# One decoder step on one core: activations written unsplit and split after reading, next round's first products between this round's, key sums queued later

## The chip, the cores and the metric

The kernel runs on one core of a Trainium2 chip. The metric is the device time of one execution in microseconds. A core has a matrix engine (TensorE, PE in the profile, whose weight loads are listed as PEld), three engines that work on tiles in on-chip memory (VectorE or DVE, ScalarE or ACT, GpSimd or POOL), and a queue that only issues transfers (SyncE, SP). Transfers (DMA) are issued from SP and, in this kernel, from ScalarE's own queue; such an issue stands in ScalarE's order like any of its instructions. Each engine works through its own list in order.

## The reference

One layer of a hybrid decoder on 2048 prompt tokens and 8 x 4 sample tokens, model width 1024:

```python
q, k, v, z, xbc, dt_raw = project(x, norm_mix, w_in)          # RMSNorm(x) @ w_in
att = three dilated window attentions, combined by their softmax denominators
ssd = ssd_mixer(z, xbc, dt_raw, ...)                          # Mamba-2 scan, gated RMSNorm
h = x + concat(att, ssd) @ w_out
gu = rmsnorm(h, norm_ffn) @ w_gate_up                         # 1024 -> 2 * 2816
y = rmsnorm(h + (silu(gu[..., :D_FF]) * gu[..., D_FF:]) @ w_down)
# sample tokens: their keys and values are the cached ones and the four new ones
sc = einsum('bshd,bsjhd->bhsj', q, k_gathered) * scale        # scores over <= 129 keys
```

It returns the two outputs and the new caches and states. All inputs and outputs are float32.

## The kernel before, in words

A float32 product is made of three faster ones. Each operand is split in two `float32r` tiles: `hi` is a rounded copy (ScalarE), `lo` the difference (VectorE), and a product is hi.hi + hi.lo + lo.hi (`mm3`, L108 to L110).

The prompt is worked in two halves of 1024 tokens. Each half runs projection, attention and scan for two blocks of 512 tokens, then the output projection, then two stages that the change touches:

1. **Rounds** (gate and up projection, `rest`, L1443 to L1476). The 2816 columns are 22 pieces `f` of 128. A piece is a 2 x 2 block product done with seven instead of eight block products: operands x11, x21, xt2, xt1, xt3, x22, xt4 (rows as `mm<-x11h` in the profile). A product is 12 matmuls (`product`, L1419). Half 0 has 22 rounds of 512 columns; half 1 also takes the sample tokens along and has 44 rounds of 264 columns, two per piece. The first two products of a round (x11 into a bank of PSUM named `mm`, x21 into one named `s`) are its lead, done by `lead_mm` at the start of the round before. `lead_ev` evacuates it: ScalarE copies x11 into `e[0]` (L1438), VectorE adds x21 (L1439), ScalarE applies SiLU (L1440). The tile `ev` has four parts, e0 to e3, and its pool has two buffers. `rest` does the other five: t2 onto the same `mm` bank, copied to e1 (L1449); t1 into a bank `o`, copied to e3 (L1453); t3 onto `mm` (L1456 adds it to e3, L1457 copies it to e2); 22 onto `o` (L1461, SiLU L1462, product L1463); t4 into a bank `t` (L1467, L1468). PSUM has two banks of each name. At the end `ev` is split (L1472 hi, L1473 lo) and both halves are written to memory as `hiD` and `loD` (L1475) from ScalarE's queue. Between the products, weights of the next pieces are split (`split_unit`, L1378, L1379).

2. **Down projection** (`down`). The 22 rows of `w_down` come in groups `g` of 2, 2, 3, 3, 3, 3, 3, 3. While group g is multiplied, group g+1's activations are read back from `hiD` and `loD` (L1505) and its weights are loaded and split (`split`, L1510 hi, L1511 lo). A group goes over 8 blocks `i` of 128 tokens, two banks each (`t` and `o`); VectorE adds each into `acc` (L1614), in group 0 ScalarE copies (L1616). Tiles of the activations are used again two groups later, so a load for g+1 waits for the end of g-1.

In half 0 the sample tokens' scan and attention run between the blocks of the down projection (`sample_parts`): every block gives credits, eight credits run one step. The steps of a branch are eight keys, one set of weights, eight values. A key step (`keys`, one sample sequence) multiplies cached keys by the broadcast query rows on GpSimd (L1003, 1024 numbers per partition), adds the halves of each head on GpSimd (L1005, 512 numbers) and sums the rest on VectorE (L1006). `weights` then transposes the scores on TensorE (L1014) and makes the softmax. The tiles `sk` come from a pool of eight (`SLOTS`); their loads, from the cache and from `qD`, are issued on ScalarE's queue.

The order on each engine is not the order of the source: a scheduler with its own cost model puts the instructions in an order when the program is built, source order being its priority. `behind(...)` (L122) and `issue_after` tie an instruction behind others in that order.

Of the kernel before, what the change touches and what calls it, by code (L numbers as in the profile page):

```python
# [8 lines left out]
F = mybir.dt.float32  # L9
R = mybir.dt.float32r  # L10
# [23 lines left out]
def hybrid_step(ctx: ExitStack, tc: tile.TileContext, x_prompt, x_sample, cache_kv_d1, cache_kv_d4,  # L34
# [34 lines left out]
    hiD = dram.tile([DFF, 2, TQ + NS // 2], F, name="hiD")  # L69
    loD = dram.tile([DFF, 2, TQ + NS // 2], F, name="loD")  # L70
# [762 lines left out]
    def sample_steps():  # L833
# [164 lines left out]
        def keys(br, b):  # L998
            def f(kvp, sm):
                nk = (128, 128, 64)[br]  # L1000
                kt, qb = W.pop((0, br, b))
                kk = kt[:, 0:1].to_broadcast([128, 4, 256]) if br == 0 else kt[:nk]
                nc.gpsimd.tensor_tensor(qb[:nk], qb[:nk], kk, op=OP.mult)  # L1003
                q4 = qb[:nk].rearrange("p s (h d) -> p s h d", h=4)
                nc.gpsimd.tensor_tensor(q4[:, :, :, :32], q4[:, :, :, :32], q4[:, :, :, 32:], op=OP.add)  # L1005
                nc.vector.tensor_reduce(sT[:nk, 4 * b:4 * b + 4], q4[:, :, :, :32], axis=mybir.AxisListType.X, op=OP.add)  # L1006
            return f

# [86 lines left out]

        yield ssd_pre
# [21 lines left out]
        for br in range(3):  # L1118
            for b in range(8):
                yield use(keys(br, b))  # L1120
            yield weights(br)
            for b in range(8):
                yield use(values(br, b))
# [35 lines left out]
    def half_step(half, X, right):  # L1159
# [265 lines left out]
        def lead_mm(r):  # L1425
            f, c0, n = r
            a11, a12 = U["a", f]
            b1 = bank("mm")
            product(b1, a11, "11", c0, n, True)
            b2 = bank("s")  # L1430
            product(b2, a12, "21", c0, n, True)
            U[r] = b1, b2

        def lead_ev(r):
            f, c0, n = r
            b1, b2 = U[r]
            ev = evp[0].tile([128, 4, TQ], F, name="ev")
            nc.scalar.copy(ev[:, 0, :n], b1[:, :n])  # L1438
            nc.vector.tensor_add(ev[:, 0, :n], ev[:, 0, :n], b2[:, :n])  # L1439
            nc.scalar.activation(ev[:, 0, :n], ev[:, 0, :n], AF.Silu)  # L1440
            U[r] = ev, b1

        def rest(j, between):  # L1443
            f, c0, n = r = rounds[j]
            s2, s1, s3, s4, a22 = U["b", f]
            ev, b1 = U.pop(r)
# [7 lines left out]
            between()  # L1454
            product(b1, s3, "t3", c0, n, False)
            v = nc.vector.tensor_add(e[3], e[3], b1[:, :n])  # L1456
            a = nc.scalar.copy(e[2], b1[:, :n])  # L1457
            with behind([v.ins, a.ins] if j == len(rounds) - 1 else ()):
                between()
            product(b3, s4, "22", c0, n, False)  # L1460
# [10 lines left out]
            hi, lo = ev[:, 0:2, :n], ev[:, 2:4, :n]  # L1471
            nc.scalar.activation(hi.bitcast(R), lo, AF.Copy)  # L1472
            nc.vector.tensor_tensor(lo.bitcast(R), lo, hi, op=OP.subtract)  # L1473
            for t, p in ((hiD, hi), (loD, lo)):
                dma2.dma_start(t[128 * f:128 * f + 128, :, c0:c0 + n], p)  # L1475
# [4 lines left out]
        def down_load(g):  # L1480
# [9 lines left out]
            def load():  # L1490
                for j in range(n):
# [12 lines left out]
                    for t, d in zip(a, (hiD, loD)):  # L1504
                        asked[:] = [dma.dma_start(t.bitcast(F).rearrange("p (b t) -> p b t", b=2),  # L1505
                                                  d[128 * f:128 * f + 128, :, :TQ]).ins]
# [18 lines left out]
            return ([load] + first if g == 1 else first + [load]), [lambda j=j: split(j) for j in range(n)], out  # L1525
# [28 lines left out]
        for k in range(2):  # L1554
            lead_ev(rounds[k])
        for j, r in enumerate(rounds):
# [5 lines left out]
            if 0 < j < len(rounds) - 1:  # L1562
                lead_mm(rounds[j + 1])
                lead_ev(rounds[j + 1])
# [17 lines left out]
            act = rest(j, between)  # L1582
# [18 lines left out]
        def down(g, ws, nw, after=None):  # L1601
            for f in nw[0]:
                f()
            for i in range(8):
# [4 lines left out]
                for nh in range(2):  # L1609
# [3 lines left out]
                    if g:  # L1613
                        add = nc.vector.tensor_add(acc[i][:, ns], acc[i][:, ns], ps)  # L1614
                    else:
# [168 lines left out]
```

## Time and profile before

| | us |
|---|---|
| median of the runs (3163.44 to 3173.74) | 3168.82 |
| profiled execution, device time | 3155.93 |
| its span, first to last instruction | 3154.2 |
| TensorE busy | 3007.1 (95%) |
| VectorE, ScalarE, GpSimd busy | 1759.6, 1285.3, 501.4 |

In the profile the rounds of half 0 run from about 815 to 1237 us, its down projection from there to 1600; the rounds of half 1 from 2388 to 2886, its down projection to the end. TensorE's time is nearly the kernel's time, so the page is read for where TensorE stands still and what ended each wait. A busy TensorE can still be slow: the granted clock (1.00 is 2.4 GHz) says at which speed it ran.

### The profile page before, as it was taken

What the parts mean: (1) busy time and instruction counts of PE and PEld (TensorE: products, weight loads), DVE (VectorE), ACT (ScalarE), POOL (GpSimd) and SP (SyncE); (2) the same over time, 40 slices, a digit from 0 to 9 for tenths busy, and PEclk for the clock granted to TensorE, in tenths of its full rate; (3) what the DMA queues carried; (4) which work ended last, traced back from release to release, by engine and by line L of the source; (5) the groups of instructions that cost most, each with busy time, mean ns of one, the idle gap of its engine ahead of it and who ended that gap; (6) DMA issues with size and microseconds to landing.
All of it is one profiled execution on the core that took longest, in us unless ns stands there. A gap on an engine that the chain in (4) does not pass through costs nothing.

```text
span 3154.2 us, 47095 instructions
## 1 busy us (share of the span) xinstructions
PE 3007.1 (95%) x18563; PEld 2498.9 (79%) x18563; DVE 1759.6 (56%) x3381; ACT 1285.3 (41%) x2636; POOL 501.4 (16%) x371
## 2 busy tenths in 40 slices
PE   7999999999999998988999999999998999999999
PEld 7889877787678787666676788777777999998777
DVE  3359623786665653644443596237856565663434
ACT  3466424663444443211144564246634444443001
POOL 1000100012332320045330000000013222220101
PEclk9899999999999999889999999999998999999999
DMA  4333444352344346559545344443433343335432
GB/s 131 93 85 108 155 133 121 89 168 98 114 147 147 134 152 245 161 181 304 139 158 145 84 117 147 148 131 90 148 113 107 118 129 125 105 106 202 151 136 102
DMA packets 457570, 431.31 MB, mean 137 GB/s; under 512 B 55652, under 2 KB 383996, under 8 KB 456836
## 3 DMA queue, kind: packets, MB, share of 16 engines
q1 hardware_dynamic: 295216, 260.02, 26.6%
q10 hardware_dynamic: 162132, 168.28, 16.8%
q8 instruction: 146, 2.39, 0.3%
q14 instruction: 76, 0.62, 0.1%
HBM read 346.14 MB, written 109.22 MB: 144 GB/s over the span
## 4 chain that ended last, share of the span: by engine, by line
PE 56%; DMA 6%; DVE 6%; POOL 4%; ACT 2%; issue 2%; ACTq 0%; POOLq 0%; DVEq 0%; SPq 0%
PE mm L1419 9%; PE o L1419 6%; PE mm L110 4%; PE mm L108 4%; PE mm L109 4%; PE t L1419 3%; PE s L1419 3%; PE t L108 2%; PE t L109 2%; PE t L110 2%; PE o L109 2%; PE o L108 2%; PE o L110 2%; DMA loD<-ev 2%; POOL sk L1003 1%
## 5 line engine op out<-in xcount | busy, mean ns | idle before, releaser
L108 PE MATMUL mm<-xh,hi 128*128 128x512 f32 (+1 forms) x1280 | 467.2, 365 | 3.0 <-ACT xh L147 2.4
L110 PE MATMUL mm<-xh,lo 128*128 128x512 f32 (+1 forms) x1280 | 463.0, 362 | 1.1 <-DVE lo L95 1.1
L109 PE MATMUL mm<-xl,hi 128*128 128x512 f32 (+1 forms) x1280 | 459.8, 359 | 1.0 <-DVE xl L148 1.0
L95 DVE TENSOR_TENSOR lo<-raw,hi 128x1024 fp32r<-128x1024 f32 x200 | 247.3, 1237 | 233.3 <-ACT hi L94 232.6
L94 ACT ACTIVATE hi<-raw 128x1024 fp32r<-128x1024 f32 x200 | 211.1, 1057 | 299.3 <-PE mm L109 121.9
L108 PEld LDWEIGHTS mm<-xh,hi 128*128 128x128 f32 x1280 | 245.2, 192 | 41.0 <-issue 7.5
L110 PEld LDWEIGHTS mm<-xh,lo 128*128 128x128 f32 x1280 | 244.6, 191 | 39.5 <-issue 4.9
L109 PEld LDWEIGHTS mm<-xl,hi 128*128 128x128 f32 x1280 | 245.4, 192 | 35.7 <-issue 3.4
L711 POOL TENSOR_TENSOR sq<-sq,acc 128x512 f32<-128x512 f32 (+2 forms) x25 | 35.6, 1425 | 1228.9 <-ACT acc L710 645.6
L1614 DVE TENSOR_TENSOR acc<-acc,t 128x512 f32<-128x512 f32 x112 | 76.7, 685 | 116.0 <-PE t L110 115.8
L591 DVE SCALAR_TENSOR_TENSOR acc<-u,cw,acc 128x512 f32<-128x512 f32 x168 | 125.6, 747 | 3.6 <-ACT acc L589 1.8
L1614 DVE TENSOR_TENSOR acc<-acc,o 128x512 f32<-128x512 f32 x112 | 76.6, 684 | 84.6 <-PE o L110 84.5
L108 PE MATMUL mm<-hi,xh 128*128 128x256 f32 (+3 forms) x408 | 115.5, 284 | 0.7 <-ACT vt L481 0.7
L110 PE MATMUL mm<-hi,xl 128*128 128x256 f32 (+3 forms) x408 | 116.0, 285 | 0.0
L109 PE MATMUL mm<-lo,xh 128*128 128x256 f32 (+3 forms) x408 | 115.9, 284 | 0.0
L356 ACT ACTIVATE p<-p,st 128x256 f32<-128x256 f32 (+4 forms) x192 | 83.8, 440 | 62.6 <-DVE st L354 56.1
L1472 ACT ACTIVATE ev<-ev 128x528 fp32r<-128x528 f32 (+1 forms) x66 | 51.8, 784 | 121.8 <-DVE ev L1468 112.6
L1620 POOL TENSOR_TENSOR acc<-acc,hr 128x1024 f32<-128x1024 f32 x16 | 40.0, 2498 | 351.7 <-DVE acc L1614 340.4
L1510 ACT ACTIVATE hi<-raw 128x1024 fp32r<-128x1024 f32 x22 | 23.0, 1059 | 170.6 <-DVE acc L1614 101.8
L1473 DVE TENSOR_TENSOR ev<-ev 128x528 fp32r<-128x528 f32 (+1 forms) x66 | 65.2, 988 | 39.2 <-ACT ev L1472 38.3
L1456 DVE TENSOR_TENSOR ev<-ev,mm 128x264 f32<-128x264 f32 (+1 forms) x66 | 33.8, 513 | 89.9 <-PE mm L1419 86.1
L108 PE MATMUL o<-hi,ah 128*128 128x512 f32 x176 | 72.2, 410 | 7.6 <-DVE acc L1614 7.6
(565 smaller groups left out, 8222.3 us busy)
## 6 DMA issues: line engine op xcount, KB each, us to landing
raw<-in_w_in SPq DMA_DIRECT2D x152, 512.0 KB
raw<-in_w_out SPq DMA_DIRECT2D x48, 512.0 KB
raw<-in_w_gate_up SPq DMA_DIRECT2D x44, 512.0 KB
sum<-in_w_gate_up SPq DMA_DIRECT2D x44, 512.0 KB
raw<-in_w_down SPq DMA_DIRECT2D x44, 512.0 KB
bc<-acD ACTq DMA_DIRECT2D x32, 384.0 KB
hiD<-ev ACTq DMA_DIRECT2D x44, 264.0 KB
loD<-ev ACTq DMA_DIRECT2D x44, 264.0 KB
```

The source lines that it names most:

```text
L94: nc.scalar.activation(h, raw, AF.Copy)
L95: nc.vector.tensor_tensor(l, raw, h.bitcast(F), op=OP.subtract)
L108: nc.tensor.matmul(ps, sh, mh, start=i == 0, stop=False)
L109: nc.tensor.matmul(ps, sh, ml, start=False, stop=False)
L110: last = nc.tensor.matmul(ps, sl, mh, start=False, stop=i == n - 1)
L356: nc.scalar.activation(p[:, h, :nk], p[:, h, :nk], AF.Exp, bias=stt[:, h:h + 1], accum_out=stt[:, 4 + h:5 + h])
L591: nc.vector.scalar_tensor_tensor(acc, u(j), w(j), acc, op0=OP.mult, op1=OP.add)
L1419: last = nc.tensor.matmul(ps[:, :n], s[:, k], m[:, k, cs], start=start and k == 0 and s is w[0] and m is x[0], stop=k == 3 and s is w[1], ...
L1472: nc.scalar.activation(hi.bitcast(R), lo, AF.Copy)
L1473: nc.vector.tensor_tensor(lo.bitcast(R), lo, hi, op=OP.subtract)
L1614: add = nc.vector.tensor_add(acc[i][:, ns], acc[i][:, ns], ps)
L1620: nc.gpsimd.tensor_tensor(acc[i], acc[i], hr, op=OP.add)
```

## The change

There are three parts. (1) `ev` is no longer split at a round's end: its parts e2 and e3 are written once, as `gD`. In the down projection they are read into the tile that will hold `lo`, and a new function `split_a` splits them in place: ScalarE copies to `hi` (L1521), VectorE subtracts in `lo` (L1522). (2) The lead of the next round is cut in two. Its x11 with the copy to e0 (L1450) stands in the source before this round's t3, its x21 with the sum (L1453) and SiLU (L1454) before this round's 22, instead of both at the start of the round. (3) A key step's sum over half heads on GpSimd is gone. VectorE sums all 64 numbers of a head (L1012, 1024 numbers per partition), two key steps later, and behind the last addition to `acc`; after the eight keys come two steps for the last sums and an empty one.

```diff
-    hiD = dram.tile([DFF, 2, TQ + NS // 2], F, name="hiD")
-    loD = dram.tile([DFF, 2, TQ + NS // 2], F, name="loD")
+    gD = dram.tile([DFF, 2, TQ + NS // 2], F, name="gD")
...
                 nc.gpsimd.tensor_tensor(qb[:nk], qb[:nk], kk, op=OP.mult)
-                q4 = qb[:nk].rearrange("p s (h d) -> p s h d", h=4)
-                nc.gpsimd.tensor_tensor(q4[:, :, :, :32], q4[:, :, :, :32], q4[:, :, :, 32:], op=OP.add)
-                nc.vector.tensor_reduce(sT[:nk, 4 * b:4 * b + 4], q4[:, :, :, :32], axis=mybir.AxisListType.X, op=OP.add)
+                late.append((sT[:nk, 4 * b:4 * b + 4], qb[:nk].rearrange("p s (h d) -> p s h d", h=4)))
+                if len(late) > 2:
+                    rest_of_keys(kvp, sm)
...
+        def rest_of_keys(kvp, sm):
+            with behind(S["adds"]):
+                nc.vector.tensor_reduce(*late.pop(0), axis=mybir.AxisListType.X, op=OP.add)
...
                 yield use(keys(br, b))
+            yield rest_of_keys
+            yield rest_of_keys
+            yield pause
             yield weights(br)
...
             nc.scalar.copy(e[3], b3[:, :n])
             between()
+            ahead(0)
             product(b1, s3, "t3", c0, n, False)
...
                 between()
+            ahead(1)
             product(b3, s4, "22", c0, n, False)
...
-            hi, lo = ev[:, 0:2, :n], ev[:, 2:4, :n]
-            nc.scalar.activation(hi.bitcast(R), lo, AF.Copy)
-            nc.vector.tensor_tensor(lo.bitcast(R), lo, hi, op=OP.subtract)
-            for t, p in ((hiD, hi), (loD, lo)):
-                dma2.dma_start(t[128 * f:128 * f + 128, :, c0:c0 + n], p)
+            dma2.dma_start(gD[128 * f:128 * f + 128, :, c0:c0 + n], ev[:, 2:4, :n])
...
-                    for t, d in zip(a, (hiD, loD)):
-                        asked[:] = [dma.dma_start(t.bitcast(F).rearrange("p (b t) -> p b t", b=2),
-                                                  d[128 * f:128 * f + 128, :, :TQ]).ins]
+                    asked[:] = [dma.dma_start(a[1].bitcast(F).rearrange("p (b t) -> p b t", b=2),
+                                              gD[128 * f:128 * f + 128, :, :TQ]).ins]
+
+            def split_a(j):
+
+                hi, lo = out[j][0]
+                nc.scalar.activation(hi, lo.bitcast(F), AF.Copy)
+                nc.vector.tensor_tensor(lo, lo.bitcast(F), hi.bitcast(F), op=OP.subtract)
...
-            return ([load] + first if g == 1 else first + [load]), [lambda j=j: split(j) for j in range(n)], out
+            return ([load] + first if g == 1 else first + [load]), [lambda j=j, f=f: f(j) for j in range(n) for f in (split_a, split)], out
...
-            if 0 < j < len(rounds) - 1:
-                lead_mm(rounds[j + 1])
-                lead_ev(rounds[j + 1])
...
+            def ahead(k):
+                if j and j + 1 < len(rounds):
+                    lead_mm(rounds[j + 1], k)
+                    lead_ev(rounds[j + 1], k)
+
+            act = rest(j, between, ahead)
```

Where the instructions stand. First ScalarE in a round of half 1, before: the end of one round and the copies of the next (`ev<-mm` and `ev<-o` are copies out of PSUM, `hi` and `lo` weight splits).

```order
L1440 ACTIVATE ev<-ev 128x264
L1472 ACTIVATE ev<-ev 128x2x264
L1475 DMA hiD<-ev 256x1x264
L1475 DMA loD<-ev 256x1x264
L1449 COPY ev<-mm 128x264
L1378 ACTIVATE hi<-sum_23300 128x512
L1438 COPY ev<-mm 128x264
L1453 COPY ev<-o 128x264
```

The same place after (one round; `out<-in_cache_kv_d` is a copy of a cache):

```order
L1477 ACTIVATE ev<-ev 128x264
L1375 DMA out<-in_cache_kv_d 16x3968
L1486 DMA gD<-ev 256x1x264
L1462 COPY ev<-mm 128x264
L1389 ACTIVATE hl<-sum_23645 128x512
L1466 COPY ev<-o 128x264
L1389 ACTIVATE hl<-sum_23647 128x512
L1450 COPY ev<-mm 128x264
L1389 ACTIVATE hl<-raw 128x512
L1471 COPY ev<-mm 128x264
```

The copy that opens the next round's buffer (L1438, now L1450) moved behind the running round's copies from `mm` (e1) and `o` (e3); one write of the old round stands between its last SiLU and these copies. TensorE beside it, before, in a round where few matmuls stand between t2 and t3:

```order
L1419 MATMUL mm<-xt2l,hl 128x264
L1419 MATMUL mm<-xt2h,hl 128x264
L1419 MATMUL o<-x22h,hl 128x264
L1419 MATMUL o<-x22l,hl 128x264
L1419 MATMUL o<-x22h,hl 128x264 x2
L1419 MATMUL o<-x22l,hl 128x264
L1419 MATMUL mm<-xt3h,hl 128x264
L1419 MATMUL mm<-xt3l,hl 128x264
```

After, in the tightest kind of round, the next round's x11 stands there:

```order
L1430 MATMUL mm<-xt2h,hl 128x264
L1430 MATMUL mm<-x11h,lo 128x264
L1430 MATMUL mm<-x11l,lo 128x264
L1430 MATMUL mm<-x11h,lo 128x264 x2
L1430 MATMUL mm<-x11l,lo 128x264
L1430 MATMUL mm<-x11h,lo 128x264 x2
L1430 MATMUL mm<-x11l,lo 128x264
L1430 MATMUL mm<-x11h,lo 128x264 x2
L1430 MATMUL mm<-x11l,lo 128x264
L1430 MATMUL mm<-x11h,lo 128x264
L1430 MATMUL mm<-xt3h,hl 128x264
L1430 MATMUL mm<-xt3l,hl 128x264
```

At least the 12 matmuls of one product now stand between t2's end and t3's start. Second, VectorE at the first branch's keys in half 0's down projection (`sT<-sk` are key sums), before:

```order
L1006 TENSOR_REDUCE sT<-sk 128x16
L1614 TENSOR_TENSOR acc_11197<-acc_11197,t 128x512
L1006 TENSOR_REDUCE sT<-sk 128x16
L1614 TENSOR_TENSOR acc_11197<-acc_11197,o 128x512
L1006 TENSOR_REDUCE sT<-sk 128x16
L1614 TENSOR_TENSOR acc_11198<-acc_11198,t 128x512
L1006 TENSOR_REDUCE sT<-sk 128x16
L1614 TENSOR_TENSOR acc_11198<-acc_11198,o 128x512
L1006 TENSOR_REDUCE sT<-sk 128x16
L1614 TENSOR_TENSOR acc_11199<-acc_11199,t 128x512
```

After:

```order
L1012 TENSOR_REDUCE sT<-sk 128x16 x2
L1633 TENSOR_TENSOR acc_11132<-acc_11132,t 128x512
L1633 TENSOR_TENSOR acc_11132<-acc_11132,o 128x512
L1012 TENSOR_REDUCE sT<-sk 128x16
L1633 TENSOR_TENSOR acc_11133<-acc_11133,t 128x512
L1633 TENSOR_TENSOR acc_11133<-acc_11133,o 128x512
L1012 TENSOR_REDUCE sT<-sk 128x16 x2
L1522 TENSOR_TENSOR x11h<-x11h 128x1024
L1633 TENSOR_TENSOR acc_11134<-acc_11134,t 128x512
```

Sums and additions stood in turn; now one or two sums stand behind each pair of additions, and an activation split (`x11h<-x11h`) among them. Third, VectorE at the start of a group of half 1's down projection, before:

```order
L1511 TENSOR_TENSOR lo<-raw,hi 128x1024
L1614 TENSOR_TENSOR acc_26297<-acc_26297,t 128x512
L1614 TENSOR_TENSOR acc_26297<-acc_26297,o 128x512
L1614 TENSOR_TENSOR acc_26298<-acc_26298,t 128x512
L1614 TENSOR_TENSOR acc_26298<-acc_26298,o 128x512
L1511 TENSOR_TENSOR lo<-raw,hi 128x1024
L1614 TENSOR_TENSOR acc_26299<-acc_26299,t 128x512
L1614 TENSOR_TENSOR acc_26299<-acc_26299,o 128x512
```

After (`al` are activations):

```order
L1527 TENSOR_TENSOR lo<-raw,hi 128x1024
L1633 TENSOR_TENSOR acc_26098<-acc_26098,t 128x512
L1522 TENSOR_TENSOR al_26446<-al_26446,ah_26445 128x1024
L1633 TENSOR_TENSOR acc_26098<-acc_26098,o 128x512
L1522 TENSOR_TENSOR al_26451<-al_26451,ah_26450 128x1024
L1633 TENSOR_TENSOR acc_26099<-acc_26099,t 128x512
L1633 TENSOR_TENSOR acc_26099<-acc_26099,o 128x512
L1633 TENSOR_TENSOR acc_26100<-acc_26100,t 128x512
L1633 TENSOR_TENSOR acc_26100<-acc_26100,o 128x512
L1527 TENSOR_TENSOR lo<-raw,hi 128x1024
```

Two activation splits now stand behind the group's first two additions.

## Rows read from the trace of the kernel before

**Rows 1.** Stages: us, TensorE, PEld, DVE, ACT, POOL busy (x), clock, DMA share, GB/s
```profile
815.00:1237.00 422.00, 417.55 (x1791) 336.31 (x1790) 241.37 (x296) 180.64 (x296) 118.71 (x80) 1.00 0.45 152
1237.00:1262.00 25.00, 16.27 (x63) 12.59 (x62) 3.83 (x4) 8.51 (x16) 0.00 (x0) 0.80 0.91 345
1360.00:1540.00 180.00, 151.92 (x733) 111.30 (x732) 77.93 (x146) 18.81 (x40) 104.72 (x54) 0.90 0.83 252
2409.00:2876.00 467.00, 438.91 (x3534) 433.64 (x3533) 277.65 (x458) 195.24 (x435) 110.92 (x80) 0.99 0.37 120
2892.00:3150.00 258.00, 254.70 (x1197) 195.72 (x1195) 112.90 (x158) 38.60 (x55) 24.98 (x17) 1.00 0.41 146
```

**Rows 2.** TensorE's waits, half 1's rounds: us in total, times, longest
```profile
PE mm L1419 <- ACT ev L1449: 17.2, 11, 2.7
PE o L1419 <- ACT ev L1453: 8.2, 5, 5.4
```

**Rows 3.** The chain in half 1's last rounds: start, us, what
```profile
2855.83 1.45 PE mm L1419 x12
...
2862.65 8.54 DMA loD<-ev
...
2871.27 0.39 ACT ev L1438
...
2872.88 3.01 PE o L1419 x12
```

**Rows 4.** ScalarE's waits, half 1's rounds
```profile
ACT ev L1438 <- DMA loD<-ev: 31.6, 29, 6.3
```

**Rows 5.** Timeline at a round's end in half 1: start, us, instruction
```profile
2858.78 0.43 DVE L1461 TENSOR_TENSOR ev<-ev,o 128x264 f32<-128x264 f32 x1 [0.94 <-PE o L1419]
2859.70 0.44 DVE L1463 TENSOR_TENSOR ev<-ev 128x264 f32<-128x264 f32 x1 [0.49 <-ACT ev L1462]
...
2861.91 0.52 ACTq L1475 DMA_DIRECT2D hiD<-ev  x1
```

**Rows 6.** Timeline of ScalarE at the crossing in half 0
```profile
1254.72 0.59 ACT L1616 COPY acc<-o 128x512 f32<-128x512 f32 x1 [11.19 <-DMA raw<-in_w_down]
```

**Rows 7.** Waits of three engines in half 0's down projection
```profile
PE o L108 <- DVE acc L1614: 15.5, 6, 4.0
PE t L1014 <- DVE sT L1006: 9.6, 3, 4.2
...
DVE sT L1006 <- POOL sk L1005: 59.0, 20, 7.3
...
POOL sk L1003 <- DMA sk<-qD: 31.2, 5, 10.1
```

**Rows 8.** Single lines: ns at least, median, most; first and last start
```profile
L1003 POOL TENSOR_TENSOR sk<-sk x24: 2347/2388/3329, 1368.9 to 1521.3; 128x1024 f32<-128x1024 f32 x16, 64x1024 f32<-64x1024 f32 x8
L1005 POOL TENSOR_TENSOR sk<-sk x24: 1249/1282/2153, 1371.4 to 1526.0; 128x512 f32<-128x512 f32 x16, 64x512 f32<-64x512 f32 x8
L1006 DVE TENSOR_REDUCE sT<-sk x24: 669/686/687, 1372.7 to 1527.3; 128x16 f32<-128x512 f32 x16, 64x16 f32<-64x512 f32 x8
L1510 ACT ACTIVATE hi<-raw x22: 1041/1062/1074, 1237.2 to 3088.6; 128x1024 fp32r<-128x1024 f32 x22
L1511 DVE TENSOR_TENSOR lo<-raw,hi x22: 1205/1221/2816, 1238.5 to 3089.7; 128x1024 fp32r<-128x1024 f32 x22
L1614 DVE TENSOR_TENSOR acc<-acc,t x112: 668/687/690, 1270.6 to 3144.7; 128x512 f32<-128x512 f32 x112
```

**Rows 9.** The chain in half 0's down projection
```profile
1474.39 4.88 DMA x11h<-hiD
1479.33 9.34 DMA el<-loD
```

**Rows 10.** Timeline of ScalarE at the crossing in half 1
```profile
2885.26 1.06 ACT L1510 ACTIVATE x21h<-raw 128x1024 fp32r<-128x1024 f32 x1
```

More of the change, by code (lines that the diff above doesn't have):

```diff
@@ L1003, in f @@
                 nc.gpsimd.tensor_tensor(qb[:nk], qb[:nk], kk, op=OP.mult)
-                q4 = qb[:nk].rearrange("p s (h d) -> p s h d", h=4)
-                nc.gpsimd.tensor_tensor(q4[:, :, :, :32], q4[:, :, :, :32], q4[:, :, :, 32:], op=OP.add)
-                nc.vector.tensor_reduce(sT[:nk, 4 * b:4 * b + 4], q4[:, :, :, :32], axis=mybir.AxisListType.X, op=OP.add)
-            return f
+                late.append((sT[:nk, 4 * b:4 * b + 4], qb[:nk].rearrange("p s (h d) -> p s h d", h=4)))
+                if len(late) > 2:
+                    rest_of_keys(kvp, sm)
+            return f
+        late = []
+        def rest_of_keys(kvp, sm):
+            with behind(S["adds"]):
+                nc.vector.tensor_reduce(*late.pop(0), axis=mybir.AxisListType.X, op=OP.add)
         def weights(br):
@@ L1094, in values, with pause @@
             return f
+        def pause(kvp, sm):
+            pass
         yield ssd_pre
@@ L1423, in half_step, with lead_mm, lead_ev, rest @@
         evp = [None]
-        def lead_mm(r):
+        def lead_mm(r, k=None):
             f, c0, n = r
[L1427 to L1434, printed above, removed]
-            f, c0, n = r
[L1436 to L1443, printed above, removed]
+            U.setdefault(r, [])
+            for j in (0, 1) if k is None else (k,):
+                b = bank(("mm", "s")[j])
+                product(b, U["a", f][j], ("11", "21")[j], c0, n, True)
+                U[r].append(b)
+        def lead_ev(r, k):
+            f, c0, n = r
+            if k == 0:
+                ev = evp[0].tile([128, 4, TQ], F, name="ev")
+                U["ev", r] = ev
+                nc.scalar.copy(ev[:, 0, :n], U[r][0][:, :n])
+            else:
+                e = U["ev", r][:, 0, :n]
+                nc.vector.tensor_add(e, e, U[r][1][:, :n])
+                nc.scalar.activation(e, e, AF.Silu)
+        def rest(j, between, ahead):
             f, c0, n = r = rounds[j]
             s2, s1, s3, s4, a22 = U["b", f]
-            ev, b1 = U.pop(r)
+            ev, b1 = U.pop(("ev", r)), U.pop(r)[0]
             e = [ev[:, k, :n] for k in range(4)]
@@ L1553, in half_step @@
         prep_rest(0)
-        for k in range(2):
-            lead_ev(rounds[k])
+        for r in rounds[:2]:
+            for k in range(2):
+                lead_ev(r, k)
         for j, r in enumerate(rounds):
@@ L1580, in between @@
                     x[0](*x[1:])
-            act = rest(j, between)
+            def ahead(k):
[3 more added lines that the diff above has]
+            act = rest(j, between, ahead)
             if j % 3 == 0:
@@ L1614, in down @@
                         add = nc.vector.tensor_add(acc[i][:, ns], acc[i][:, ns], ps)
+                        S["adds"] = [add.ins]
                     else:
```

## The prediction

> **What bounds the kernel now.** I read the stage table first (windows cut at the stages of both halves), then what TensorE waited for in each stage, then the chain of waits at the worst places, and last single lines. The device time of the profiled execution is 3155.93 us around a span of 3154.2; the median of the runs shown is 3168.82, 12.9 us (0.4%) longer. The sum below is made against the profiled execution and its difference is then set off from the median.
>
> The reader is to see in the stage table [rows 1] that TensorE is busy nearly all the time, so what can be won is its idle time, and that three stages hold most of that: half 1's rounds (467.0 - 438.91 = 28.1 us), half 0's key and value stretch inside the down projection (180.0 - 151.92 = 28.1 us, at a granted clock of 0.90) and the crossing from half 0's rounds into its down projection (25.0 - 16.27 = 8.7 us). Half 0's rounds lose 4.5 us, half 1's down stage 3.3, most of that at its very end, with VectorE busy 112.9 of 258 us. The change touches all five.
>
> In half 1's rounds TensorE waits for ScalarE's copies out of PSUM: 17.2 us for the first one (e1, which the product t3 accumulates onto) and 8.2 for the second (e3) [rows 2]. Why ScalarE is late stands in the chain [rows 3]: the write of `loD` took 8.54 us, the copy L1438 that opens the next round's buffer started when it had landed, and TensorE's x22 product started 1.6 us after that. `ev` has two buffers, so round j+1 overwrites what round j-1 is still writing out; ScalarE works in its own order, and the copies for the running round stand behind L1438. It stood 31.6 us for that in 29 of the rounds [rows 4].
>
> **The change part by part.** *Rounds, half 1.* Per round one ScalarE and one VectorE split go (44 of each here) and one of two writes, so the buffer is free earlier. More important, L1438 now stands behind e1 and e3 of the running round, and TensorE has a product of the next round to do before t3 and another before x22. In the order as built, 7 of half 1's 44 rounds had only 4 or 5 matmuls between t2's end and t3's start and 19 had just 12; now 8 have 12 and the other 36 at least 17. A product of 12 takes 1.45 us [rows 3]. What can be late next: the write to `gD` is issued on ScalarE's queue ahead of the next round's e1 copy, and waits for the end of the old round. From VectorE's e1 sum to the end of its product took 1.36 us (2858.78 to 2860.14), an issue 0.52 [rows 5], the copy itself about as long as L1438's 0.39 [rows 3]: 2.3 us, against two products, 2.9 us, in the tightest order. One weight split of VectorE between them makes it some 0.4 us late; 8 rounds x 0.4 = 3 us. So -28.1 + 3 = -25 us. Bounds: -28 (nothing waits) and 0 (the copies are late for another reason).
>
> *Rounds, half 0.* Same mechanism with products twice as long: -3.5 of 4.5 us.
>
> *Crossing in half 0.* TensorE waited there for the evacuation of the down stage's first group, which ScalarE did after standing 11.19 us, a DMA released it [rows 6], at a DMA share of 0.91 [rows 1]. Of the activation traffic queued there, half goes: in the orders, twelve loads of 512 KB become six. Those are 3.1 MB at the 345 GB/s of that stretch, 9 us of transfer; only what is queued ahead of the blocked rows counts, and new splits stand in ScalarE's way (g=1's splits are ahead of the first evacuation). I take half of the idle time, -4; bounds 0 and -8.7.
>
> *Keys in half 0's down stage.* A key cost GpSimd 2.39 + 1.28 us [rows 8], and VectorE stood 59.0 us for GpSimd with the sums of the down projection queued behind it, so TensorE waited 15.5 us for those sums and 9.6 for the transposes of the scores [rows 7]. A block i of a three-row group is 18 matmuls at 254.7/1197 = 0.213 us [rows 1], 3.83 us, and gives 15 credits of which a step takes 8: a step is 2.04 us of TensorE. Eight keys: 16.3 us of TensorE against 29.4 of GpSimd, 13 short in each of three branches, 39 us; 28.1 were idle. Now GpSimd needs 8 x 2.39 = 19.1 us, and eight keys, two late sums and the pause give 11 steps, 22.5 us. So GpSimd no longer falls behind; what stays is that it waited 31.2 us for loads of q rows [rows 7]. The activation loads that compete for that stretch are halved. VectorE's sum over 64 instead of 32 numbers costs between 0.69 (no more) and 1.37 us (twice) [rows 8]; I take 1.2, near a split's 1.22 of the same 1024 numbers, 12 us over 24 sums on an engine busy 77.93 of 180 us. Nine more steps make 92 (I counted 83 yields before) against 85 that the credits pay for (17 rows x 8 blocks x 5 / 8), so the last seven run in a lump ahead of the last group: small matmuls, whose loads are long asked for; cost 0 to 3 us, taken inside the next number. I keep 12 of the 28.1 us idle: -16; bounds 0 and -28. The clock: 0.90 granted over 180 us, with levels of 1.2 and 2.4 GHz, is 36 us at the lower one; 28 were idle, so at least 8 us of matmuls ran at half speed, 4 us lost. Of those and the slow starts after each wait, -3.
>
> The row says of the sharing of GpSimd and VectorE: a VectorE split took 1.22 us in the median and 2.816 at worst, a GpSimd product 2.39 and 3.329 [rows 8]. The Trainium skill, "SBUF — State Buffer", section "Who interferes with whom", has the rule that speaks against this change: a VectorE instruction with two SBUF inputs and a GpSimd one that reads SBUF exclude each other for a whole instruction, and a sum over one input does not. By that rule the new activation splits are the kind that collides, about eleven of them beside the keys, up to 1.6 us each by the worst row: 18 us more of VectorE and a sum of -25 if none were hidden, in place of -43. By the rows' medians it is nothing, and the removed half-width sums on GpSimd collided as well.
>
> *Activation splits in the down stage.* 22 splits of 128x1024 per half, 1.06 us on ScalarE and 1.22 on VectorE each [rows 8], in place of loads that went straight to TensorE. By busy time they fit: 27 us more of VectorE on 112.9 of 258. The price is in the queues. A load is asked for when its tile comes free at a group's start; the split stands just behind the group's first sum, and all later sums stand behind the split on VectorE, the evacuations behind it on ScalarE. Landing took 4.88 us in one row and 9.34 in another, in the crowded stretch of half 0 [rows 9]. With 4.88: 4.88 + 1.06 + 1.22 + 0.69 for the sum [rows 8] = 7.9 us, and TensorE wants that bank at 5 x 9 x 0.213 = 9.6 us: covered. With 9.34: 12.3 us, 2.7 us late, and two more splits in line (2 x 1.22) make it 5. Fourteen groups: 0 to 70 us. Half 1's down stage had little traffic (0.41 [rows 1]), so I use 4.88 there and take three late half-0 groups of 2 us, +6.
>
> *Crossing in half 1.* Behind t3 stand now four splits, not two; ScalarE's first began at 2885.26 [rows 10]. Two more at 1.22 us on VectorE are 2.4 us that only two 1.45 us products could cover, and those cover the first two: +2.5. In half 0 the products are 2.8 us long and cover all four: 0.
>
> Sum: -25 - 3.5 - 4 - 16 - 3 + 6 + 2.5 = -43 us. 3155.9 - 43 = 3112.9; from the median 3168.8 - 43 = **3126 us**.
>
> **The rivals.** *All of it pays (0.14).* No wait is left in the rounds, and the loads come in time since half their bytes are gone: -28 - 4.5 - 8.7 - 28 - 4 + 2.5 = -71, 3098 us. For it: GpSimd's time per branch is now under TensorE's. Against: the 31.2 us that GpSimd waited for loads.
>
> *The waits move inside ScalarE's queue (0.12).* Each round's write stands ahead of the next round's e1 copy on ScalarE, and if VectorE's queue (weight splits, 0.69 us) makes the old round's end late in every tight and half-tight place, half 1's rounds win 10 and not 25; if GpSimd's loads also stay the bound, the keys win 6: -43 + 15 + 10 = -18, 3151 us. For it: 1.36 of the 2.3 us were taken with nothing queued in between.
>
> *No change (0.04).* The idle time of both big stages turns out to be the loads' own (they fill 0.83 of the key stretch and 0.37 of the rounds); the low share in the rounds speaks against it: 3165.
>
> *Slower (0.08).* The activation split blocks VectorE and ScalarE at every group's start, in both halves. Place: the split behind the first sum of a group; price: 5 us x 14 = 70 in place of 6, so -43 + 64 = +21, 3190 us. It decides from 49/14 = 3.5 us of TensorE per group, which a landing of about 8 us with three splits in line gives. For it: 9.34 us was seen. Against: half 1's weights go through the same load, copy and subtraction in the same queues, and TensorE was busy 254.7 of 258 us there [rows 1].
>
> **How the numbers follow.** Forecast 0.62, the rivals 0.14, 0.12, 0.04 and 0.08. Within 0.3% (9.5 us) is what a measurement of this kernel can't tell from no change. The forecast's own range, 3108 to 3145, follows from half the bounds of the keys, the rounds and the splits together; with the rivals on both sides the range for 8 in 10 is 3097 to 3161. Faster by over 0.3%: 0.62 + 0.14 and 0.10 of the third = 0.86; within: 0.06; slower: 0.08.
>
> **What would show it.** Right: no line of waits of TensorE for L1462 or L1466 (the copies) over 2 us in total in half 1's rounds, its idle time there at 3 to 6 us; VectorE's waits for GpSimd in the key stretch well under 59 us, and that stretch at a clock near 1; 66 writes fewer. Wrong: TensorE waiting for sums (L1633) at group starts in half 1's down stage, with VectorE behind L1522 and ScalarE behind a load of `gD`.

## Result: 3092.43 us, and the profile after

| | before | after |
|---|---|---|
| median of the timed runs | 3169.72 us (3163.44 to 3173.74, 4 runs) | 3092.43 us (3086.47 to 3098.17, 4 runs) |
| profiled execution | 3155.93 us | 3098.17 us |
| TensorE busy, idle in its span | 3007.1, 147.1 us | 2988.4, 108.0 us |
| bytes moved by DMA | 431.31 MB | 384.78 MB |

The ratio is 0.9758, 95% interval 0.9731 to 0.9785: 77 us faster, where 43 were forecast. One execution among the experiments, of the kernel with late sums, took 10046 us and is left out of that kernel's numbers.

The stages of the changed kernel, in windows that answer to [rows 1] (half 0's rounds, their crossing, the key stretch, half 1's rounds, half 1's down projection):

```profile
815.00:1227.00 412.00, 412.00 (x1778) 333.46 (x1777) 203.36 (x272) 158.68 (x273) 115.81 (x80) 1.00 0.39 123
1227.00:1252.00 25.00, 19.64 (x83) 14.70 (x82) 8.43 (x10) 13.84 (x23) 0.00 (x0) 0.96 0.84 298
1345.00:1510.00 165.00, 150.19 (x720) 112.43 (x718) 103.38 (x137) 26.75 (x39) 74.12 (x30) 0.92 0.75 223
2380.00:2814.00 434.00, 431.69 (x3540) 430.43 (x3540) 246.51 (x416) 172.62 (x394) 110.12 (x80) 1.00 0.32 100
2834.00:3092.00 258.00, 255.06 (x1186) 196.47 (x1186) 131.83 (x174) 54.82 (x70) 25.88 (x17) 0.99 0.30 100
```

Half 1's rounds have 2.3 us of idle left of 28.1, half 0's none. But they became shorter by more than that: TensorE's busy time fell too, from 438.91 to 431.69 us for the same work (3534 and 3540 matmuls stand in the two windows). Part of this is TensorE's clock, granted at 0.99 there before and 1.00 after. A place in the control, a second profile of the kernel before (below), shows it. TensorE stands for the copy e1, and soon after the end of that wait the granted clock is 0.50, the lower of its two levels (1.2 GHz): 18 matmuls in 3.40 us, where the next 3.40 us at full clock hold 30.

```profile
2637.93 0.28 PE L1419 MATMUL o<-x22l,lo 128*128 128x264 f32 x1
2640.84 0.39 PE L1419 MATMUL mm<-xt3h,hi 128*128 128x264 f32 x1 [2.63 <-ACT ev L1449]
...
2642.40:2645.80 3.40, 3.40 (x18) 3.40 (x17) 2.20 (x6) 1.18 (x3) 0.00 (x0) 0.50 0.26 91
2645.80:2649.20 3.40, 3.40 (x30) 3.40 (x29) 1.96 (x4) 1.07 (x2) 0.00 (x0) 1.00 0.02 5
```

From its first to its last e1 copy in half 1 the control spent 17.1 us at the lower level by the trace's records of the clock, 13.7 of them with TensorE busy; the changed kernel spent 0.7. What TensorE still waits for in half 1's rounds, against the 17.2 and 8.2 us of [rows 2]:

```profile
PE mm L1430 <- ACT ev L1450: 1.4, 3, 0.5
PE mm L1430 <- ACT ev L1462: 0.9, 2, 0.6
```

In half 0's down stage VectorE waits 11.9 us for GpSimd (59.0 in [rows 7]), while GpSimd's own wait for q rows has grown from 31.2 to 89.3: it is now ahead of its loads. The stretch is not free of waits, though. TensorE still stands 6.4 us for key sums (9.6 before), and 14.8 of the 165 us of its row are idle.

```profile
DVE sT L1012 <- POOL sk L1002: 11.9, 7, 2.3
PE t L1019 <- DVE sT L1012: 6.4, 3, 3.2
POOL sk L1002 <- DMA sk<-qD: 89.3, 12, 32.3
```

The table cuts both traces at the same instructions (the first and last e1 copy of a half, its first evacuation and its first and last add, by their starts in the timeline; the down projection of half 1 to the end). The control is a second profile of the kernel before, below.

| stretch | forecast | after less before | after less control |
|---|---|---|---|
| half 0: first to last e1 copy | -3.5 | -10.0 | -10.9 |
| half 0: last e1 copy to first add | -4 | -1.8 | -3.2 |
| half 0: first to last add | -16 - 3 + 6 = -13 | -22.5 | -19.5 |
| half 0's last add to half 1's first e1 copy (the change isn't there) | 0 | +6.5 | -6.2 |
| half 1: first to last e1 copy | -25 | -33.8 | -36.8 |
| half 1: last e1 copy to first evacuation | +2.5 | +4.8 | +4.0 |
| half 1: down projection | 0 | +0.2 | +0.8 |
| span | -43 | -57.7 | -73.3 |

The first two rows share a border that moved. The last round's t1 product, 12 matmuls, stood ahead of the last e1 copy and now stands behind it (1725 and 1712 matmuls in that stretch). At 412/1778 = 0.232 us each, some 2.8 us of the first row belong to the second.

### The profile page after: what moved, and what is told of

It is laid out like the page before. It is cut to its first block, busy times and chain, and to the rows that moved or that the text cites. A ratio compares the mean times of both kernels' runs of the same rounds, so it can differ in the third digit from the quotient of the medians.

```text
span 3096.4 us, 46767 instructions
## 1 busy us (share of the span) xinstructions
PE 2988.4 (97%) x18563; PEld 2490.0 (80%) x18563; DVE 1760.7 (57%) x3359; ACT 1282.5 (41%) x2614; POOL 470.7 (15%) x347
## 2 busy tenths in 40 slices
DMA packets 427647, 384.78 MB, mean 124 GB/s; under 512 B 53892, under 2 KB 370972, under 8 KB 426916
## 4 chain that ended last, share of the span: by engine, by line
PE 62%; DMA 5%; DVE 4%; ACT 2%; POOL 1%; issue 1%; ACTq 0%; POOLq 0%; SPq 0%; DVEq 0%
PE mm L1430 11%; PE o L1430 8%; PE mm L109 5%; PE mm L107 5%; PE mm L108 5%; PE t L1430 4%; PE s L1430 4%; PE t L107 2%; PE t L109 2%; PE t L108 2%; PE o L107 2%; PE o L108 2%; PE o L109 2%; DMA sk<-qD 1%; DMA out<-ko 1%
## 5 line engine op out<-in xcount | busy, mean ns | idle before, releaser
L93 ACT ACTIVATE hi<-raw 128x1024 fp32r<-128x1024 f32 x200 | 211.0, 1057 | 296.0 <-PE mm L108 121.9
L107 PE MATMUL t<-hi,ah 128*128 128x512 f32 x176 | 75.2, 427 | 2.0 <-DVE acc L1633 2.0
L107 PEld LDWEIGHTS mm<-hi,xh 128*128 128x128 f32 (+1 forms) x408 | 74.8, 184 | 1.7 <-ACT vt L480 1.0
L108 PEld LDWEIGHTS mm<-lo,xh 128*128 128x128 f32 (+1 forms) x408 | 74.9, 184 | 0.9
```

Of the source, the lines that this page charges most:

```text
L93: nc.scalar.activation(h, raw, AF.Copy)
L107: nc.tensor.matmul(ps, sh, mh, start=i == 0, stop=False)
L108: nc.tensor.matmul(ps, sh, ml, start=False, stop=False)
```

## Experiments

All times are medians, the ratio is to the kernel before on the same chip, with its 95% interval. "Won in the rounds" means half 1's first to last e1 copy, against the control's 473.8 us.

**Control.** `-from contextlib import ExitStack` / `+from contextlib import ExitStack  # control`

> The kernel before with one comment added. Theory 'offset': the profiled execution of before (3155.9) happened to lie 14 us under the timed ones, so a second profiled execution gives 3163 to 3174 and a ratio of 1.000; then about 14 of the 77 us won are no work of the change's terms but the base they were subtracted from. Rival 'profiling': a profiled execution is always 10 to 15 us under the timed ones, so the new one is near 3156 again.

3170.89 us, ratio 1.0006 [0.9992, 1.002]; its profiled execution took 3171.50. So "offset" holds: the profile that I subtracted from lay 14 us under the timed runs by chance. 12.7 of the 15.6 us between the two profiles lie between half 0's last add and half 1's first round, which the change does not touch. There TensorE is busy 9.8 us longer for the same 4823 matmuls, at a lower granted clock; first the profile of before, then the control, and last the control's half 1's rounds, as in [rows 1]:

```profile
1613.90:2408.10 794.20, 764.02 (x4823) 608.74 (x4824) 468.12 (x992) 389.59 (x810) 54.03 (x45) 0.98 0.42 126
1613.50:2420.50 807.00, 773.79 (x4823) 615.64 (x4824) 468.17 (x992) 390.25 (x810) 54.46 (x46) 0.97 0.43 124
2421.00:2891.00 470.00, 441.84 (x3536) 436.84 (x3535) 277.97 (x458) 195.37 (x435) 110.58 (x80) 0.98 0.37 119
```

**One part at a time: lead, spill.**

```
lead:   lead_mm, lead_ev, rest(.., ahead) as in the change; hiD/loD and the keys as before
spill:  -  for t, p in ((hiD, hi), (loD, lo)): dma2.dma_start(t[...], p)
        +  dma2.dma_start(gD[...], ev[:, 2:4, :n])     and split_a in the down stage
```

> Only the lead products of the next round and their copies are moved between this round's products; the activation is still split before it is written, in two writes, and the keys are as before. Theory 'order' (the copies e1 and e3 stood behind the copy that waits for the ev buffer): half 1's rounds lose 25 to 32 us by this alone, half 0's rounds 3, total 3135 to 3145. Rival 'buffer' (what counts is how long the two writes hold the buffer): the wait moves to the lead copy, TensorE then waits for the next round's first sums, and half 1's rounds win under 10: 3155 to 3165.

> Only the unsplit write and the split after the read back; lead and keys as before. Theory 'order': half 1's rounds win 5 to 12 us (the buffer is free earlier, but e1 still stands behind the copy that waits), crossing of half 0 -4, half 1's down 0; total 3148 to 3160. Rival 'buffer': half 1's rounds win 20 to 28, total 3130 to 3140. Third: if fewer loads beside the key stretch free GpSimd's q loads, half 0's down wins 5 to 10 more.

Lead: 3163.36 us, 0.9988 [0.9976, 1.0]; the rounds won 0.4 us. Spill: 3158.98, 0.997 [0.9953, 0.9986]; they won 12.7. Theory "order" falls: the moved lead alone gains nothing there. "Buffer" falls too, by the spill, which should have won 20 to 28 us in these rounds and 30 to 40 in all. In half 0's rounds the lead alone won 6.8 us against the control's 407.9, and the spill alone lost 8.0; neither was forecast, and the loss is not traced further. Half 0's down stage did not gain by the spill (347.8 us, 340.2 in the control).

With the lead, the waits of half 1's rounds have only changed their name. TensorE hardly waits for e1 any more, but for the lead's own copy (L1439 in this kernel), and that for the buffer; first TensorE's row, then ScalarE's:

```profile
PE mm L1419 <- ACT ev L1439: 24.5, 9, 3.6
PE mm L1419 <- ACT ev L1451: 2.5, 2, 1.6
...
ACT ev L1439 <- DMA loD<-ev: 38.0, 25, 3.6
```

With the spill alone e1 still stands behind the copy that waits (L1437), in the old order:

```profile
PE mm L1418 <- ACT ev L1448: 10.4, 6, 2.4
PE o L1418 <- ACT ev L1452: 8.2, 7, 1.9
...
ACT ev L1437 <- DMA gD<-ev: 64.9, 24, 6.0
```

**The two together, without the keys.**

> The unsplit write and the moved lead together, keys as before. Each alone changed the time by under 9 us (lead 3163, spill 3159). Theory 'both' (the moved lead copy itself still waits for the buffer, now in TensorE's way, unless the buffer is free earlier): half 1's rounds lose 30 to 37 us against the control, half 0's rounds 8 to 11, total 3115 to 3125. Rival 'keys too' (the keys part shares the gain): rounds win under 20, total 3135 to 3145.

3115.61 us, 0.9846 [0.9816, 0.9877]; the rounds won 37.8 us. "Both" holds: 0.9988 x 0.997 would be 0.9958 (-13 us), measured is -49. Some 36 us come from neither part alone.

**What of the spill it takes: bytes or the split.** One kernel keeps the split and halves the write; the other drops the split and doubles the write.

```
lead_w1:        -  for t, p in ((hiD, hi), (loD, lo)):
                +  for t, p in ((hiD, hi),):
spill_lead_w2:  +  dma2.dma_start(gE[...], ev[:, 2:4, :n])    behind the same write to gD
```

> The moved lead, with the split still done before the write, but only the high part is written, and read back for both parts (so the low part of the activation is left out and its place taken by a second copy of the high part). Theory 'bytes' (the two writes of 8.5 us hold the buffer): half 1's rounds win as with both parts, 28 to 36 us, total 3118 to 3132. Rival 'split' (the two split instructions in ScalarE's and VectorE's queues hold it): half 1's rounds win under 10, total 3152 to 3162.

> The unsplit write and the moved lead, but each activation is written twice, the second time to a tensor that nobody reads. Theory 'bytes': TensorE waits again for the lead copy, some 20 us in half 1's rounds, total 3138 to 3152. Rival 'split': the rounds win as with both parts, total 3115 to 3125.

One write with the split: 3150.73 us, 0.9955 [0.9936, 0.9973], rounds -12.7. Two writes without it: 3120.96, 0.9864 [0.9835, 0.9892], rounds -33.8. The first fits neither forecast (its one write waits for the rounded copy alone, no longer for the subtraction, so it leaves earlier too). The second is "split"'s. With two writes of the same size either way, the rounds win 0.4 us with the split ahead of them and 33.8 without: bytes are not it. Where no split stands ahead, a second write costs 4 us of the rounds.

**The split on one engine.** `-nc.scalar.activation(hi.bitcast(R), lo, AF.Copy)` / `+nc.vector.tensor_copy(hi.bitcast(R), lo)` in the kernel with the lead alone.

> The moved lead, split before the write and two writes, keys as before; but both halves of the split run on VectorE (the copy too), so that ScalarE does not stand for VectorE's product and VectorE not for ScalarE's copy. Theory 'ping-pong' (the two crossings between the engines at a round's end cost the time, not the engines' busy time): half 1's rounds win 20 to 35 us against the control, total 3125 to 3140. Rival 'busy time' (0.4 to 0.7 us more work per round at the end of the chain and two issues): half 1's rounds win under 10, total 3150 to 3165.

3150.66 us, 0.9937 [0.9913, 0.9962], rounds -14.5: between the two theories and so for neither.

**A split that nobody waits for,** put into the changed kernel behind the write to `gD`.

```
dead_two:  +  nc.vector.tensor_copy(hi.bitcast(R), lo)
           +  nc.vector.tensor_tensor(hi.bitcast(R), lo, hi, op=OP.subtract)
dead_one:  two tensor_copy          dead_act:  the copy by nc.scalar.activation
```

> The changed kernel, and behind each activation's write a copy and a subtraction on VectorE into the same buffer's free half, which nobody reads (the write waits for neither). Theory 'VectorE's time' (0.6 + 0.7 us more per round, up to twice beside GpSimd, in the queue that the round's end stands in): half 1's rounds lose 12 to 22 us, total 3105 to 3120. Rival 'chain to the write' (only what stands between the last product and the landing counts): half 1's rounds lose under 4, total 3090 to 3097.

> As the last, but two copies with one input each instead of a copy and a subtraction. If the subtraction's collision with GpSimd is what costs, half 1's rounds lose under half of what the subtraction loses; if VectorE's time as such, within 4 us of the same; under 'chain to the write' under 4.

> As the first, but the copy stands on ScalarE and the subtraction on VectorE, as in the kernel before. If the crossing between the two engines costs by itself, half 1's rounds lose 8 us or more beyond the first of these three, total 3115 to 3135; if not, they lose the same or less, total 3100 to 3118; under 'chain to the write' under 4.

3093.52 us (0.9763 [0.9742, 0.9783]), 3090.50 (0.9757 [0.9741, 0.9774]) and 3096.00 (0.978 [0.9765, 0.9795]); rounds -36.5, -37.8 and -36.1, as after. So "chain to the write" holds and the other two fall: the split's time on VectorE costs nothing, nor does the crossing between engines, although in the last of the three ScalarE stands 61.2 us for it:

```profile
ACT ev L1488 <- DVE ev L1483: 61.2, 26, 3.4
```

What costs is the split's place ahead of the write. How it costs is seen only in part. From the timelines, half 1's rounds: in the median the last write's issue ended 2.35 us behind VectorE's last product of the round with the lead alone, 1.30 with one write, 1.24 with two unsplit writes, 0.56 after. From the start of that issue to the waiting copy the median is 2.59 to 2.70 us in the kernels of this table (2.82 with two unsplit writes), but the late ones differ:

| | copies that waited over 3.5 us, of those that waited for the write | TensorE's wait for the lead copy | rounds |
|---|---|---|---|
| lead | 9 of 25 | 24.5 us | -0.4 |
| lead, one write | 10 of 27 | 17.1 | -12.7 |
| lead, split on VectorE | 5 of 29 | 13.2 | -14.5 |
| spill and lead, two writes | 3 of 19 | 3.8 | -33.8 |
| after | 1 of 18 | 1.4 | -36.8 |

Of the 24.5 us with the lead alone, 12.7 came in four waits behind such late copies, and 11.8 in five whose write was issued late (its issue ended 3.2 to 7.2 us behind that product). TensorE's order is no rival here: in all five kernels 48 matmuls or more stand between x11 and its round's t2 in 33 of 44 rounds.

One of the late ones in the kernel with one write; the first row is SyncE's queue, the others ScalarE's. A load of weights is issued 0.14 us ahead of the write, and the copy waits 5.32 us from the write's issue:

```profile
2603.43 0.37 SPq L1387 DMA_DIRECT2D sum<-in_w_gate_up  x1
...
2603.57 0.53 ACTq L1478 DMA_DIRECT2D hiD<-ev  x1
...
2608.89 0.38 ACT L1438 COPY ev<-mm 128x264 f32<-128x264 f32 x1 [3.79 <-DMA hiD<-ev]
```

And after, where no load stands ahead, 2.60 us:

```profile
2615.63 0.53 ACTq L1486 DMA_DIRECT2D gD<-ev  x1
...
2618.23 0.38 ACT L1450 COPY ev<-mm 128x264 f32<-128x264 f32 x1 [1.39 <-DMA gD<-ev]
```

Whether a write issued later meets the loads more often stays open: it was not tried by moving the loads alone, several of the late ones have no load near them, and two unsplit writes end as late as one split write (1.24 and 1.30 us) with 3 of 19 copies late instead of 10 of 27. Nor does a late copy always cost: with the split behind the write on both engines 6 of 15 are late, and TensorE waits 1.8 us for them.

**The keys alone, and with the spill.** `late.append(..)` / `rest_of_keys`, without GpSimd's half add, as in the change.

> Only the key part: the half add on GpSimd goes, VectorE sums 64 numbers, two keys later, behind a sum of the down projection. Theory 'own': half 0's down stage wins 20 to 27 us by this alone, total 3142 to 3150, rounds unchanged. Rival 'loads': GpSimd then waits for q rows behind the activation loads that are not halved here, and the stage wins under 12: 3157 to 3163.

> The unsplit write and the keys, lead as before. Theory 'loads help keys' (halved activation loads give GpSimd its q rows sooner): half 0's down stage wins 20 to 24 us against the control, where keys alone won 11 there; total 3128 to 3138. Rival 'no help': the stage wins 8 to 13 as with keys alone, total 3136 to 3146.

3143.86 us, 0.9927 [0.9901, 0.9953], and 3133.67, 0.9908 [0.9877, 0.9938]. The keys are worth 23 us alone (by the ratio), 20 on top of the spill and 28 on top of spill and lead: roughly, they add up with the rest. Both totals are as "own" and "loads help keys" had them. But from half 0's first to its last add the control's 340.2 us fell to 328.5 with the keys alone, which is "loads"' number, and to 319.4 with the spill, which would be "loads help keys". Since this stretch varies by 10 us between two profiles of one kernel (below), and the profile of the keys alone was of the longest of its four executions (3154.43 us), the profiles don't settle how far the loads help.

**Which half of the keys part,** on top of spill and lead.

```
keys_nohalf:  -  nc.gpsimd.tensor_tensor(q4[..:32], q4[..:32], q4[..32:], op=OP.add)
              +  nc.vector.tensor_reduce(sT[...], q4, ...)          at once
keys_late:    half add kept, sums through late / rest_of_keys, pause
```

> Unsplit write and moved lead as after; of the keys part only GpSimd's half add goes (VectorE sums 64 numbers), and the sum is queued at once, with no extra steps. Theory 'GpSimd time' (24 half adds of 1.28 us were what the sums waited for): half 0's down stage is as short as after, 17 us below that of the unsplit write and moved lead alone; VectorE's wait for GpSimd falls from 51 to under 20 us; total 3092 to 3102. Rival 'place in the queue' (a sum queued at once stands ahead of the down projection's sums whatever GpSimd takes): the stage wins under 7, total 3108 to 3118.

> Unsplit write and moved lead as after; GpSimd's half add stays, and only the sums are queued two keys later, behind a sum of the down projection, with the three extra steps. Theory 'GpSimd time': VectorE's waits for GpSimd stay over 30 us and the stage wins under 7 us, total 3108 to 3118. Rival 'place in the queue': the stage wins 12 to 17, total 3095 to 3104.

3097.83 us, 0.978 [0.9751, 0.9809], and 3100.72, 0.9792 [0.9765, 0.9819]. By the medians of before beside them the two win 22 and 19 us over spill and lead alone, both together 28: each does most of it, so neither theory holds by itself. (The intervals are some 9 us to either side, so which of the two is worth more is not shown.) VectorE's wait for GpSimd with spill and lead alone, without the half add, and with late sums:

```profile
DVE sT L1005 <- POOL sk L1004: 51.4, 19, 5.5
```
```profile
DVE sT L1004 <- POOL sk L1002: 27.1, 14, 4.9
```
```profile
DVE sT L1014 <- POOL sk L1004: 27.5, 14, 3.1
```

**A version to beat both.** In the changed kernel VectorE once stands 4.57 us for a split that waits for its load, with the down projection's sums behind it, and TensorE 3.26 us for one of these sums:

```profile
1442.53 1.23 DVE L1522 TENSOR_TENSOR x11h<-x11h 128x1024 fp32r<-128x1024 f32 x1 [4.57 <-ACT x11h L1521]
...
1445.79 0.80 PE L107 MATMUL o<-hi,ah 128*128 128x512 f32 x1 [3.26 <-DVE acc L1633]
```

```
wfirst:    -  for j in range(n) for f in (split_a, split)
           +  for f in (split, split_a) for j in range(n)
wfirst_x:  also  -  todo[2:] = [all first[1]]
                 +  todo[1:] = [first[1][2:], first[1][:2]]
```

> The changed kernel again, on the same chip as the next two and as the kernel before: 3088 to 3098, ratio 0.974 to 0.978; half 0's down stage 16 to 22 us under the control's.

> The changed kernel, but in each group of the down stage the weights are split first and the read-back activations after them, so that a load of gD has three more blocks (some 11 us) to land. Theory 'splits at the group's start': VectorE's and ScalarE's waits for gD go, half 0's down stage loses 4 to 8 us more, total 3084 to 3092. Rival 'loads of the keys': no change of the stage beyond 2 us, 3090 to 3098. A third: the later splits come too late for the next group, and TensorE waits at group starts: 3098 to 3110.

> As the weights-first kernel, and the first group's two activation splits stand one place earlier in the last round. Theory: half 1's crossing, 4 us longer than before the change, comes back by 2 to 4 us; total 1 to 4 us under the weights-first kernel. Rival: the splits are put ahead of the round's own copies and wait there for the loads of gD, so that the last round or the one before loses 2 to 8 us.

The change again: 3092.50 us, 0.9758 [0.9737, 0.9778]. Weights first: 3087.42, 0.9747 [0.9729, 0.9765]. With the first group's splits earlier: 3095.85, 0.976 [0.9735, 0.9785]. The three can't be told apart. The crossing did come back, by 5.5 us where 2 to 4 were expected (last e1 copy to first evacuation 16.1, 15.8 and 10.3 us; control 13.1), but the total did not follow. Half 0's down stage differs by more than that between two profiles of the very same changed kernel: 320.7 and 311.1 us, the second 29 under the control where 16 to 22 were expected. Most of that spread is busy time at a lower granted clock, for the same 1613 matmuls:

```profile
1257.70:1578.40 320.70, 297.23 (x1613) 218.35 (x1611) 205.28 (x371) 77.24 (x136) 103.46 (x50) 0.94 0.59 179
1258.80:1569.90 311.10, 289.61 (x1613) 213.36 (x1611) 205.84 (x372) 77.22 (x136) 103.69 (x50) 0.97 0.61 185
```

Why one execution is granted more of the full clock than the other is not shown. A gain of 5 us is below this spread.

## Why the prediction was wrong

The direction, the stages and the waits were right, the size was not: 3126 us forecast, 3092.43 measured, under the range's low end of 3097. The rival "all of it pays" (3098) came closest in number, but not by its reasons: it had no idle time left in the key stretch (14.8 us stayed) and all 8.7 us of half 0's crossing back (some 5 to 6 came).

- *Half 1's rounds (-25).* The idle time went as the term said: 28.2 us in the control, 2.3 after. The failed step is that only idle time was summed. Busy time fell by another 10 us (441.84 to 431.69), and I had put that at nothing: slow matmuls were allowed for in the key stretch alone (-3), although [rows 1] has a clock of 0.99 for these rounds. By the clock (13.7 us of busy time at half speed in the control, 0.7 after) some 6.5 of the 10 us are matmuls that no longer run at the lower level, an estimate. The rest fits the last matmul before each wait, which is booked with its whole 0.28 us (the row at 2637.93) where the next one otherwise starts after 434/3540 = 0.12; this was not tried by itself. Half 0's rounds won 10.9 us: 5.2 were idle in the control, 2.8 only moved over the border, and about 3 were busy time of this kind.
- *Where the miss lies.* The control's span fell by 30 us more than forecast: 11.8 of it in half 1's rounds, 7.4 in half 0's (2.8 of that belongs to the crossing), 6.5 in half 0's down stage, and 6.2 in a stretch that the change doesn't touch, which is luck of the two profiles.
- *The reason given for it.* "More important, L1438 now stands behind e1 and e3": alone that wins 0.4 us in half 1 (6.8 in half 0). And the write of 8.54 us in [rows 3] was a late one; from the issue of such a write of 264 KB to the copy behind it 2.6 us are usual. The Trainium skill, "DMA: Bandwidth & Descriptors", section "Anatomy of one DMA — SWDGE (gpsimd) path", gives about 2.0 us fixed plus the bytes at 436 GB/s, 2.6 us for 264 KB by estimate. It gives this for transfers issued from GpSimd; the writes here are issued from ScalarE, and the median of 2.59 us after agrees, for this one size. The gain needs both parts: the lead, so that e1 doesn't stand behind the buffer, and a write that doesn't wait for a split, so that the lead doesn't either. I had added up parts that multiply.
- *Keys (-16, and -3 for the clock).* 20 to 28 us by the timed runs: a little small. I put it on GpSimd's time alone; the place of the sum in VectorE's queue does as much. The split between idle and slow time was off as well: of the 19.5 us that half 0's first to last add lost against the control, 9.9 are idle time and 9.7 busy time (306.9 to 297.2). The clock in the key stretch rose to 0.92, not near 1.
- *Activation splits (+6).* In half 1 nothing, as forecast: its down stage took as long as before with 131.83 instead of 112.90 us on VectorE, and no sum is waited for there. The +6 were put on half 0. There the spill without the keys changed the down stage by +7.6 us (lead as before) and, with the lead, by -2.7 (340.4 to 337.7), within the spread of this stretch, so the term is not settled. The slower rival's mechanism occurs (the rows at 1442.53 and 1445.79) but not in every group.
- *Crossings.* Half 1 +2.5, measured +4 to +4.8; half 0 -4, measured -1.8 to -3.2, or -4.6 to -6.0 with the moved product.
- *The base.* 14 us: the one profile of before was a short execution. I set the sum off from the median, so this is no error of the sum, but the stage differences to that profile come out 15.6 us too small, as the control shows.
- *The rule that spoke against the change* (the Trainium skill, "SBUF — State Buffer", section "Who interferes with whom") would have made the sum -25. The collisions are there (below); the stage they fall in still won more than forecast, so what they cost is not visible there.

## What to carry to other kernels

Where engines' queues and a buffer's return both hold a wait, removing one only renames it: look in the trace for what the next instruction in that queue would wait for, and change both. Sum what TensorE loses around a wait by comparing a matmul's cost in an undisturbed stretch with the stage's whole length, not by its idle time: busy time after a wait can be at the lower clock. Profile the kernel before twice before subtracting stages, and compare the granted clock of the two.

## What the runs showed of the hardware

A subtraction with both inputs in SBUF takes about twice as long on VectorE while GpSimd multiplies; a sum over one input and an add from PSUM do not. After the change, GpSimd (first row) and VectorE in the same stretch:

```profile
1357.08 10.43 POOL L1002 TENSOR_TENSOR sk<-sk 128x1024 f32<-128x1024 f32 x4 [2.29 <-DMA sk<-qD]
...
1361.88 1.22 DVE L1012 TENSOR_REDUCE sT<-sk 128x16 f32<-128x1024 f32 x1 [1.14 <-POOL sk L1002]
1363.01 2.27 DVE L1522 TENSOR_TENSOR x11h<-x11h 128x1024 fp32r<-128x1024 f32 x1
1365.20 0.67 DVE L1633 TENSOR_TENSOR acc<-acc,t 128x512 f32<-128x512 f32 x1
```

Over the whole trace a split (L1522) has a median of 1.22 us away from GpSimd's work and 2.40 where it overlaps a product or an addition of GpSimd (7 of 44); all 24 sums lie within 0.02 us of each other:

```profile
L1012 DVE TENSOR_REDUCE sT<-sk x24: 1201/1211/1221, 1350.1 to 1510.0; 128x16 f32<-128x1024 f32 x16, 64x16 f32<-64x1024 f32 x8
```

The Trainium skill, "SBUF — State Buffer", section "Who interferes with whom", says that a VectorE instruction with two SBUF inputs contends with a GpSimd one that reads SBUF, and that one with at most one SBUF input does not. The trace agrees. So moving the half add from GpSimd into VectorE's sum also took away a partner of those collisions.
